# Feed-forward products as single float32 instructions in a one-core encoder layer

## The chip, the cores and the metric

The kernel runs on one NeuronCore of a Trainium2 chip. The metric is the device time of one execution in microseconds (us). TensorE (PE) multiplies matrices, VectorE (DVE), ScalarE (ACT) and GpSimd (POOL) do the rest of the arithmetic, and SyncE (SP) issues most of the transfers between device memory and the on-chip SBUF. Each engine works through its own queue in order.

## The reference

One layer of a bidirectional encoder is computed for two sequences of 1024 rows with 1024 features, all in float32. Attention (four heads with low-rank compressed queries, keys and values) and a two-dimensional Fourier mixing run side by side on one normalised input. The change lies in what follows, the gated feed-forward part:

```python
x = x + ga1 * mix
h2 = rmsnorm(x, g_ffn) * (1.0 + sc2) + sh2
ffn = (jax.nn.silu(h2 @ w_gate) * (h2 @ w_up)) @ w_down
return x + ga2 * ffn
```

`w_gate` and `w_up` are 1024 x 2816, `w_down` is 2816 x 1024. A last normalisation of the rows follows.

## The kernel before

**How a product is written.** A float32 matrix is split into a rounded half `hi` (ACT casts it to float32r, line 63) and a remainder `lo` (DVE subtracts, line 64). `mm3` (lines 78 to 81) then adds three matmuls into one PSUM bank: hi x hi, hi x lo and lo x hi. Nearly all products of the kernel are made this way. In a few places, such as `fold_out` (line 322), a product of two plain float32 tiles is one `matmul`.

**Order.** Each engine's instructions are put in order by a scheduler that follows the dependencies; `tc.issue_after` and `first` add orders by hand, and `behind()` (line 71) holds an instruction until the last split has been issued. Tiles with the same tag share memory: a load into one waits until the last reader of its predecessor has finished.

**Feed-forward (from line 1544).** Both products use a seven-product scheme on 2 x 2 blocks (Strassen's, in Winograd's form), so sums of blocks are multiplied instead of eight plain block pairs. It works in two stages for each of the two sequences.

- *Gate and up* (the loop over `order`, 22 iterations). The seven right-hand sides, `H[k]`, are blocks of the transposed input or sums of them, each 128 x 4 x 512. They stay in SBUF for the whole stage, as a hi and a lo tile. `prep_h` loads each as plain float32 into a staging tile (`HSTAGE`, line 1550) and splits it. The seven left-hand sides of an iteration come from `combos`: it loads two tiles of 512 KB from `wgu` into slots of the tag X (four of them, line 1556), and `sums_w` (line 1622) makes three new tiles and changes one in place, with four subtractions: t3, then b12 and t2, then t4. They are on POOL except in the first iterations. `hl` splits each of the seven. `prod` (line 1767) runs four `mm3` for each pair, 28 in an iteration. Between them DVE and ACT read the three PSUM banks `x`, `y` and `z` of the iteration, apply silu and multiply. `put_s` stores the results and sums of them to device memory (`s_d`); in the first sequence `down_combos` makes sums of `w_down` (`t_d`).
- *Down* (`prod2`, line 1938). Seven calls with eleven steps each. A step loads two 128 x 512 tiles into an X slot from `s_d` and from `w_down` or `t_d`, splits both, and runs four `mm3` into four banks. Between the steps, `hooks` run the residual, the last normalisation and the loads and splits of the next sequence's `H`. In the second sequence the seventh product is prepared ahead: `prep_last` loads and splits its eleven pairs into the memory of `H`, and 44 `mm3` at line 2067 follow.

That gives 2 x 22 x 28 = 1232 products in the first stage, 13 x 11 x 4 = 572 in the second and the 44 at line 2067: 1848 products of a 128 x 128 by a 128 x 512 tile.

**The entry.** While the last rows of attention's output projection run, `prep_h` loads the first `H` tiles, splits are placed among the projection's own DVE and ACT work with `issue_after` and `first` (lines 1660 to 1674), and the first weight sums go to DVE into the tile `H41`, unused at that time.

Of the kernel before, what the change touches and what calls it, by code (L numbers as in the profile page):

```python
# [12 lines left out]
F32 = mybir.dt.float32  # L13
# [8 lines left out]
P = 128  # L22
# [13 lines left out]
VALS = 18  # L36
# [17 lines left out]
def hybrid_encoder_kernel(ctx: ExitStack, tc: tile.TileContext, a: dict):  # L54
# [1489 lines left out]
    with ExitStack() as st:  # L1544
# [5 lines left out]
        HSTAGE = (("H20", "H21", "H30", "H31", "H20", "H21", "X0"), ("H20", "H21", "H30", "H31", "H30", "H20", None))  # L1550

# [3 lines left out]
        def slot(i, name="draw"):  # L1555
            return w.tile([P, 2, 512], F32, tag=f"X{i % 4}", name=name, bufs=1)


        for tag in ("H20", "X0", "X1", "H21", "H30", "H31", "H00", "H41", "H01", "H50", "H51", "H10", "H11", "H40", "H60", "H61"):
            quad(tag) if tag[0] == "H" else [slot(2 * int(tag[1]) + i) for i in range(2)]  # L1560

        def prep_h(H, s, n):

            raw = {}

            def load(i):
                k = HK[i]
                src = h2_d[s][:, HSRC[k][0] : HSRC[k][0] + 4, 512 * HSRC[k][1] : 512 * HSRC[k][1] + 512] \
                    if isinstance(HSRC[k], tuple) else hc_d[s][:, :, HSRC[k], :]
                if HSTAGE[s][i] is None:  # L1570
                    raw[k] = [val() for _ in range(4)]
                    for c in range(4):
                        nc.sync.dma_start(raw[k][c], src[:, c, :])
                elif HSTAGE[s][i] == "X0":
                    raw[k] = [slot(c, "hx") for c in range(2)]
                    for c in range(2):
                        nc.sync.dma_start(raw[k][c], src[:, 2 * c : 2 * c + 2, :])
                else:
                    t = quad(HSTAGE[s][i])
                    for c in (0, 2):  # L1580
                        nc.sync.dma_start(t[:, c : c + 2, :], src[:, c : c + 2, :])
                    raw[k] = t

            ahead = 4 if s == 0 else 3
            then = {0: 4, 1: 5, 4: 6} if s == 0 else {0: 3, 1: 5, 2: 4, 3: 6}
            for i in range(ahead):
                load(i)
                if s == 1:
                    yield
                if s == 0 and i == 0:  # L1590
                    S["rgu"] = [slot(j, "rgu0") for j in range(2)]
                    for j in range(2):
                        nc.sync.dma_start(S["rgu"][j].rearrange("p a b -> p (a b)"), a["wgu"][j, 0])
                    x3_load()
            if s == 0:
                yield
            for i, k in enumerate(HK):
                H[k] = [quad(f"H{k}{j}", F32R) for j in range(2)]
                for c in range(0, 4, n):
                    if HSTAGE[s][i] is None:  # L1600
                        for cc in range(c, c + n):
                            with behind():
                                split(H[k][0][:, cc, :], H[k][1][:, cc, :], raw[k][cc])
                    else:
                        rk = raw[k][c // 2] if HSTAGE[s][i] == "X0" else raw[k][:, c : c + n, :]
                        with behind() if s == 1 else ExitStack():
                            split(H[k][0][:, c : c + n, :], H[k][1][:, c : c + n, :], rk)
                    if c + n == 4:
                        raw.pop(k)
                        if i in then:  # L1610
                            load(then[i])
                    yield
# [44 lines left out]
        prep = prep_h(H, 0, 2)  # L1657
        next(prep)
        r, wc = S.pop("rgu"), quad("H41")
        after_a, after_v = S.pop("tail")  # L1660
        with tc.issue_after(after_a), tc.issue_after(after_v):
            next(prep)
            next(prep)
            first(here["a"], S.pop(("tail", 5)))
            first(here["v"], S.pop(("tail", 6)))
            first(here["v"], S.pop(("tail", 2)))
            first(here["v"], S["tail", 4])
            first(here["a"], S.pop(("tail", 7)))
        with tc.issue_after(S.pop(("tail", 4))):
            w0 = sums_w([r[i // 2][:, i % 2, :] for i in range(4)], lambda i: wc[:, i, :], nc.vector)  # L1670
            first(here["s"], S["tail", 3])
            with tc.issue_after(S.pop(("tail", 3))):
                next(prep)
                next(prep)
# [3 lines left out]

        def prep_step(n):
            with tc.issue_after(here["v"]):  # L1680
                for _ in range(n):
                    next(prep, None)

        for n in range(4):
# [3 lines left out]
            prep_step((2, 0, 0, 0)[n])  # L1688
            if n == 1:
                hts = quad("H40")  # L1690
# [16 lines left out]
        def hl(v):  # L1707
            h = w5.tile([P, 512], F32R, tag="wh", name="wh", bufs=8)
            if "gf" not in S:
                S["gf"] = w5.tile([P, D], F32, name="gf")  # L1710
                w5.tile([P, 2, 512], F32, tag="ga", name="tdb", bufs=1)
            l = w5.tile([P, 512], F32R, tag="wl", name="wl", bufs=8)
            split(h, l, v)
            return h, l

        gf, first_w = None, None
        order = [fi + half * (NF // 2) for fi in range(NF // 2) for half in range(2)]
        pending = []
        turn = [0]
        for s in range(2):  # L1720
            def combos(n, first=False, ahead=0):
                f = order[n]
                if first and n == 1:
                    b = [val() for _ in range(4)]
                    for i, t in enumerate(b):
                        nc.sync.dma_start(t, a["wgu"][i // 2, f][:, 4 * (i % 2) : 4 * (i % 2) + 4, :].rearrange("p c m -> p (c m)"))
                    return b
                r = [slot(turn[0] + ahead + i, "rgu") for i in range(2)]
# [3 lines left out]
                b = [r[i // 2][:, i % 2, :] for i in range(4)]  # L1732
                return b if n == 1 and s == 1 else sums_w(b, lambda i: val(), nc.vector if n == 0 else nc.gpsimd)
# [13 lines left out]
            def down_combos(f):  # L1747
                wd_ = a["w_down"]
                b1 = w5.tile([P, 2, 512], F32, tag="ga", name="tdb", bufs=1)
# [43 lines left out]
            if s == 0:  # L1793
                wts = [hl(w0[i]) for i in range(4)]
                with behind():
                    for _ in range(2):
                        next(prep)
            else:
                wts = first_w
            A = {}  # L1800
            late = None
            for n, f in enumerate(order):
                cur, nxt = wts, []
                src = combos(n + 1, s == 0 and n == 0) if n + 1 < NF else None
# [8 lines left out]
                def step(j, ps, k, first, src=src):  # L1813
                    prod(ps, k, cur[j], first)
                    if s == 0 and n == 0:
                        if j == 0:
                            cur.extend(hl(v) for v in w0[4:])
                            w0.clear()
                            S["n3"] = norm3(1, S.pop("jk3").bitcast(BF16))
                        if j < 3:  # L1820
                            with behind():
                                for _ in range(2):
                                    next(prep, None)
                            if j == 1:
                                with behind():
                                    S.pop("n3")()
                            return
                        if j == 3:
                            src = S["w1"] = sums_w(src, lambda i: val(), nc.vector)
                        src = S["w1"]  # L1830
                        for i in ((), (), (), (0, 1), (2, 3), (4,), (5, 6))[j]:
                            nxt.append(hl(src[i]))
                        if j == 6:
                            flip2(3, [S.pop(("xn", 1, 3, u)) for u in range(2)], bank, lambda g: val())
                    elif s == 1 and n == 0:
                        if j == 2:
                            with tc.issue_after(here["u2"]):
                                S["w1"] = sums_w(src, lambda i: val(), nc.vector)
                        with behind(), tc.issue_after(here["c"]) if j > 1 else ExitStack():
                            for i in ((), (), (0,), (1, 2), (3,), (4,), (5, 6))[j]:  # L1840
# [355 lines left out]
```

## Time and profile before

| | us |
|---|---|
| median of three runs | 1994.35 (1994.21 to 1997.55) |
| the profiled execution | 1991.72 |
| its span, first to last instruction | 1989.9 |
| last matmul of the projection, first of feed-forward | about 714.5 |
| last matmul of feed-forward | about 1981 |
| memory read, written | 263.01 MB, 120.65 MB |

The span is the stretch from the first to the last instruction of the profiled execution; its time has 1.8 us more around it. In the profile, a line begins with the source line, the engine, the operation, and output <- inputs. Behind the first bar of a group stands its busy time and the mean length of one instruction in ns, behind the second the idle time of the engine just before them and what ended it. A matmul is recorded as two instructions, a weight load (PEld) and the matmul proper (PE); matmul records overlap, so the pace is read from their starts.

### The profile page before, as it was taken

What the parts mean: (1) busy time and instruction counts of PE and PEld (TensorE: products, weight loads), DVE (VectorE), ACT (ScalarE), POOL (GpSimd) and SP (SyncE); (2) the same over time, 40 slices, a digit from 0 to 9 for tenths busy, and PEclk for the clock granted to TensorE, in tenths of its full rate; (3) what the DMA queues carried; (4) which work ended last, traced back from release to release, by engine and by line L of the source; (5) the groups of instructions that cost most, each with busy time, mean ns of one, the idle gap of its engine ahead of it and who ended that gap; (6) DMA issues with size and microseconds to landing.
All of it is one profiled execution on the core that took longest, in us unless ns stands there. A gap on an engine that the chain in (4) does not pass through costs nothing.

```text
span 1989.9 us, 27639 instructions
## 1 busy us (share of the span) xinstructions
PE 1965.3 (99%) x9554; PEld 1621.7 (81%) x9554; DVE 1382.5 (69%) x2081; ACT 893.7 (45%) x1743; POOL 831.0 (42%) x1008
## 2 busy tenths in 40 slices
PE   8999999999999999999999999999999999999998
PEld 6788778888888878888888888888888888888886
DVE  5667767666777687877767668779655665656794
ACT  5764545555565563333333355443333333335551
POOL 2554012111312348977877401345644544510152
PEclk9999999999999999999999999999999999999999
DMA  9986965535354584654655597774322322357762
GB/s 392 333 318 227 358 237 116 110 91 160 101 117 138 191 283 166 218 181 172 200 182 190 171 316 231 239 230 150 133 96 90 132 94 92 116 199 241 254 228 85
DMA packets 167081, 377.12 MB, mean 190 GB/s; under 512 B 18044, under 2 KB 43260, under 8 KB 163740
## 3 DMA queue, kind: packets, MB, share of 16 engines
q1 hardware_dynamic: 144252, 304.03, 45.2%
q0 software_dynamic: 22112, 70.27, 11.4%
q8 instruction: 75, 1.23, 0.2%
q10 hardware_dynamic: 576, 1.05, 0.1%
q14 instruction: 66, 0.54, 0.1%
HBM read 263.01 MB, written 120.65 MB: 193 GB/s over the span
## 4 chain that ended last, share of the span: by engine, by line
PE 59%; DVE 2%; issue 1%; POOL 1%; DMA 1%; ACT 0%; SPq 0%; POOLq 0%; DVEq 0%; ACTq 0%
PE bank L80 20%; PE bank L79 20%; PE bank L81 20%; DVE wl L64 1%; DMA draw<-in_w_down_dram 1%; DVE val L1987 0%; DVE val L154 0%; DVE val L1878 0%; DVE H L64 0%; DMA val<-x_d 0%; POOL rs_y L107 0%; POOL val L154 0%; DVE val L151 0%; POOL out_dram L1993 0%; DVE val L1875 0%
## 5 line engine op out<-in xcount | busy, mean ns | idle before, releaser
L79 PE MATMUL bank<-H,wh 128*128 128x512 f32 x1232 | 480.2, 390 | 2.6 <-DVE val L154 0.9
L80 PE MATMUL bank<-H,wh 128*128 128x512 f32 x1232 | 479.5, 389 | 0.3 <-DVE H L64 0.3
L81 PE MATMUL bank<-H,wl 128*128 128x512 f32 x1232 | 479.3, 389 | 0.2 <-DVE wl L64 0.2
L79 PEld LDWEIGHTS bank<-H,wh 128*128 128x128 f32 x1232 | 231.2, 188 | 53.2 <-DVE val L1861 2.0
L64 DVE TENSOR_TENSOR wl<-draw,wh 128x512 fp32r<-128x512 f32 x286 | 209.0, 768 | 94.0 <-ACT wh L63 93.5
L81 PEld LDWEIGHTS bank<-H,wl 128*128 128x128 f32 x1232 | 231.3, 188 | 49.0 <-DVE wl L64 0.5
L80 PEld LDWEIGHTS bank<-H,wh 128*128 128x128 f32 x1232 | 231.3, 188 | 48.2 <-DVE H L64 0.6
L154 DVE TENSOR_TENSOR val<-bank,val 128x512 f32<-128x512 f32 x200 | 136.6, 689 | 163.0 <-PE bank L81 162.1
L63 ACT CAST wh<-draw 128x512 fp32r<-128x512 f32 x286 | 164.9, 619 | 173.2 <-PE bank L80 131.6
L154 POOL TENSOR_TENSOR val<-val 128x512 f32<-128x512 f32 x58 | 82.4, 1421 | 345.7 <-DVE val L1959 163.5
L80 PE MATMUL bank<-wl,wh 128*128 128x512 f32 x572 | 223.2, 390 | 0.8 <-DVE wl L64 0.5
L63 ACT CAST wh<-rgu 128x512 fp32r<-128x512 f32 x172 | 107.1, 623 | 258.4 <-PE bank L80 203.2
L81 PE MATMUL bank<-wh,wl 128*128 128x512 f32 x572 | 222.6, 389 | 0.0
L79 PE MATMUL bank<-wh 128*128 128x512 f32 x572 | 222.6, 389 | 0.0
L63 ACT CAST wh<-val 128x512 fp32r<-128x512 f32 x133 | 82.3, 622 | 261.9 <-PE bank L80 249.3
L64 DVE TENSOR_TENSOR wl<-val,wh 128x512 fp32r<-128x512 f32 x133 | 126.1, 950 | 65.4 <-ACT wh L63 65.3
L64 DVE TENSOR_TENSOR wl<-rgu,wh 128x512 fp32r<-128x512 f32 x172 | 162.5, 945 | 0.8 <-ACT wh L63 0.7
L151 POOL TENSOR_TENSOR val<-rgu 128x512 f32<-128x512 f32 x80 | 108.3, 1354 | 78.7 <-DMA rgu<-in_wgu_dram 74.9
L80 PEld LDWEIGHTS bank<-wl,wh 128*128 128x128 f32 x572 | 107.4, 188 | 25.2 <-DVE wl L64 2.9
L79 PEld LDWEIGHTS bank<-wh 128*128 128x128 f32 x572 | 107.4, 188 | 22.5
L81 PEld LDWEIGHTS bank<-wh,wl 128*128 128x128 f32 x572 | 107.4, 188 | 21.9
L151 POOL TENSOR_TENSOR val<-val 128x512 f32<-128x512 f32 x89 | 119.1, 1356 | 1.3
(403 smaller groups left out, 3885.5 us busy)
## 6 DMA issues: line engine op xcount, KB each, us to landing
rgu<-in_wgu_dram SPq DMA_DIRECT2D x86, 512.0 KB, 4.0
draw<-s_d SPq DMA_DIRECT2D x143, 256.0 KB, 3.4
s_d<-val POOLq DMA_DIRECT2D x88, 256.0 KB, 3.0
draw<-t_d SPq DMA_DIRECT2D x88, 256.0 KB, 4.2
s_d<-val SPq DMA_DIRECT2D x66, 256.0 KB, 3.8
draw<-in_w_down_dram SPq DMA_DIRECT2D x55, 256.0 KB, 4.1
xt<-in_x_dram SPq DMA_DIRECT2D x16, 512.0 KB, 7.3
wada<-in_w_ada_dram SPq DMA_DIRECT2D x16, 512.0 KB, 9.8
```

Source lines behind the costliest of these rows:

```text
L63: here["a"] = nc.scalar.copy(hi, src).ins
L64: here["v"] = (eng or nc.vector).tensor_tensor(out=lo, in0=src, in1=rd(hi), op=ALU.subtract).ins
L79: nc.tensor.matmul(out, lh, rh, start=first, stop=False, skip_group_check=cont)
L80: nc.tensor.matmul(out, lh, rl, start=False, stop=False, skip_group_check=cont)
L81: here["t"] = here["pe"] = nc.tensor.matmul(out, ll, rh, start=False, stop=last, skip_group_check=cont).ins
L151: return eng.tensor_tensor(out=out, in0=x, in1=y, op=ALU.subtract).ins
L154: eng.tensor_tensor(out=out, in0=x, in1=y, op=ALU.add)
```

## The change

- `prod`, `prod2` and the 44 products at line 2067 issue one `nc.tensor.matmul` on plain float32 tiles instead of `mm3` on split ones.
- `hl`, `HSTAGE` and the splits of `H`, of the weight sums and of the down operands are gone, with most of the hand-made orders around them.
- `prep_h` loads each `H` tile straight into its place; `prep_last` does the same with the eleven held pairs, two in one tile.
- The freed memory goes to eight X slots (from four), 30 `val` tiles (from 18), a second tile for `tdb`, and own tiles `wc0` and `hts`.
- `combos` makes t3 and t4 on DVE, b12 and t2 on POOL, in every iteration; b11, b21, b12 and b22 are used by TensorE from the X slots themselves.

```diff
-        def prep_h(H, s, n):
+        def prep_h(H, s):
+            for k in HK:
                 src = h2_d[s][...] if isinstance(HSRC[k], tuple) else hc_d[s][:, :, HSRC[k], :]
...
+                t = H[k] = quad(f"H{k}")
+                for c in (0, 2):
+                    nc.sync.dma_start(t[:, c : c + 2, :], src[:, c : c + 2, :])
                 yield
...
-        prep = prep_h(H, 0, 2)
+        prep = prep_h(H, 0)
         next(prep)
-        r, wc = S.pop("rgu"), quad("H41")
...
+        r = [slot(j, "rgu0") for j in range(2)]
+        for j in range(2):
+            nc.sync.dma_start(r[j].rearrange("p a b -> p (a b)"), a["wgu"][j, 0])
+        x3_load()
+        for _ in prep:
+            pass
+        S.pop("tail")
+        wc = w.tile([P, 4, 512], F32, name="wc0")
...
-                r = [slot(turn[0] + ahead + i, "rgu") for i in range(2)]
+                r = [slot(turn[0] + i, "rgu") for i in range(2)]
...
-                return b if n == 1 and s == 1 else sums_w(b, lambda i: val(), nc.vector if n == 0 else nc.gpsimd)
+                b11, b21, b12, b22 = (r[i // 2][:, i % 2, :] for i in range(4))
+                t3, t2, t4 = val(), val(), val()
+                sub(t3, b22, b12, nc.vector)
+                sub(b12, b12, b11, nc.gpsimd)
+                sub(t2, b22, b12, nc.gpsimd)
+                sub(t4, b21, t2, nc.vector)
+                return [b11, t2, b21, t3, b12, t4, b22]
...
             def prod(ps, k, wt, first):
-                wh, wl = wt
                 for c in range(4):
-                    cs = slice(c * P, c * P + P)
-                    mm3(ps, wh[:, cs], wl[:, cs], H[k][0][:, c, :], H[k][1][:, c, :], first and c == 0, c == 3, not first)
+                    here["t"] = nc.tensor.matmul(ps, wt[:, c * P : c * P + P], H[k][:, c, :], start=first and c == 0, stop=c == 3,
+                                                 skip_group_check=not first).ins
...
                     nc.sync.dma_start(raw[:, 0, :], s_d[s][k, f])
                     nc.sync.dma_start(raw[:, 1, :], bsrc(k, f))
-                    ah, al = hl(raw[:, 0, :])
-                    bh, bl = hl(raw[:, 1, :])
                     for t in range(4):
-                        tt = slice(t * P, t * P + P)
-                        mm3(ps[t], ah[:, tt], al[:, tt], bh, bl, first and f == 0, last and f == NF // 2 - 1, not first)
+                        nc.tensor.matmul(ps[t], raw[:, 0, t * P : t * P + P], raw[:, 1, :], start=first and f == 0,
+                                         stop=last and f == NF // 2 - 1, skip_group_check=not first)
```

More of the change, by code (lines that the diff above doesn't have):

```diff
@@ L35 @@
 NOUT = 6
-VALS = 18
+VALS = 30
 FF = 2816
@@ L1555, in slot @@
         def slot(i, name="draw"):
-            return w.tile([P, 2, 512], F32, tag=f"X{i % 4}", name=name, bufs=1)
-        for tag in ("H20", "X0", "X1", "H21", "H30", "H31", "H00", "H41", "H01", "H50", "H51", "H10", "H11", "H40", "H60", "H61"):
-            quad(tag) if tag[0] == "H" else [slot(2 * int(tag[1]) + i) for i in range(2)]
-        def prep_h(H, s, n):
-            raw = {}
-            def load(i):
-                k = HK[i]
+            return w.tile([P, 2, 512], F32, tag=f"X{i % 8}", name=name, bufs=1)
@@ L1568, in load @@
+        for tag in ("H0", "X0", "X1", "X2", "X3", "H5", "H1", "H6", "H4", "H3", "H2", "X4", "X5", "X6", "X7"):
+            quad(tag) if tag[0] == "H" else slot(int(tag[1]))
+        def prep_h(H, s):
+            for k in HK:
                 src = h2_d[s][:, HSRC[k][0] : HSRC[k][0] + 4, 512 * HSRC[k][1] : 512 * HSRC[k][1] + 512] \
                     if isinstance(HSRC[k], tuple) else hc_d[s][:, :, HSRC[k], :]
[L1570 to L1594, printed above, removed]
@@ L1595, in prep_h @@
-            if s == 0:
-                yield
[L1597 to L1612, printed above, removed]
+                t = H[k] = quad(f"H{k}")
@@ L1677, in hybrid_encoder_kernel @@
         norm2(1, 2, 1, xb)
[L1679 to L1682, printed above, removed]
         for n in range(4):
@@ L1705, in val, with combos @@
             return w5.tile([P, 512], F32, tag="v", name="val", bufs=VALS)
[L1707 to L1714, printed above, removed]
         gf, first_w = None, None
+        S["gf"] = w5.tile([P, D], F32, name="gf")
         order = [fi + half * (NF // 2) for fi in range(NF // 2) for half in range(2)]
         pending = []
-        turn = [0]
+        turn = [4]
         for s in range(2):
-            def combos(n, first=False, ahead=0):
+            def combos(n):
                 f = order[n]
[L1723 to L1727, printed above, removed]
-                r = [slot(turn[0] + ahead + i, "rgu") for i in range(2)]
+                r = [slot(turn[0] + i, "rgu") for i in range(2)]
                 turn[0] += 2
@@ L1748, in down_combos @@
                 wd_ = a["w_down"]
-                b1 = w5.tile([P, 2, 512], F32, tag="ga", name="tdb", bufs=1)
+                b1 = w5.tile([P, 2, 512], F32, tag="tdb", name="tdb", bufs=2)
                 nc.sync.dma_start(b1, wd_[f * P : f * P + P, :].rearrange("p (a b) -> p a b", a=2))
@@ L1791, in put_s @@
                 store_s(2, fi, v4, nc.gpsimd)
[L1793 to L1799, printed above, removed]
+            wts = w0 if s == 0 else first_w
             A = {}
@@ L1802, in hybrid_encoder_kernel @@
             for n, f in enumerate(order):
-                cur, nxt = wts, []
-                src = combos(n + 1, s == 0 and n == 0) if n + 1 < NF else None
+                cur = wts
+                wts = combos(n + 1) if n + 1 < NF else None
                 if late is not None:
@@ L1811, in hybrid_encoder_kernel, with step @@
                         comb_h(1, n // 4 - 1) if n >= 5 else None
-                def step(j, ps, k, first, src=src):
+                def step(j, ps, k, first):
                     prod(ps, k, cur[j], first)
@@ L1816, in step @@
                         if j == 0:
-                            cur.extend(hl(v) for v in w0[4:])
-                            w0.clear()
                             S["n3"] = norm3(1, S.pop("jk3").bitcast(BF16))
[L1820 to L1832, printed above, removed]
+                        if j == 1:
+                            S.pop("n3")()
                         if j == 6:
                             flip2(3, [S.pop(("xn", 1, 3, u)) for u in range(2)], bank, lambda g: val())
[L1835 to L1840, printed above, removed]
-                                nxt.append(hl(S["w1"][i]))
-                        if j == 6:
-                            S.pop("w1")
-                    elif src is not None:
-                        nxt.append(hl(src[j]))
-                    if s == 0 and n == 1 and j == 2:
-                        S.pop("w1", None)
                 def pend():
                     if pending:
-                        with behind():
-                            pending.pop(0)()
+                        pending.pop(0)()
                 x, y, z = bank(), bank(), bank()
@@ L1897, in prep_last @@
             def prep_last():
-                tags = ("H00", "H01", "H50", "H51", "H10", "H11", "H60", "H61", "H40", "H41", "H30")
-                raw = {}
-                def load(f):
-                    raw[f] = quad(("H21", "H31", "H20")[f % 3])
-                    nc.sync.dma_start(raw[f][:, 0, :], s_d[1][2, f])
-                    nc.sync.dma_start(raw[f][:, 1, :], bsrc(2, f))
-                for f in range(2):
-                    load(f)
-                    yield
-                for f, tag in enumerate(tags):
-                    if f + 2 < len(tags):
-                        load(f + 2)
-                    yield
-                    q = quad(tag, F32R)
-                    for i in range(2):
-                        with behind():
-                            split(q[:, 2 * i, :], q[:, 2 * i + 1, :], raw[f][:, i, :])
-                        if i == 0:
-                            yield
-                    raw.pop(f)
-                    held.append(q)
+                for f in range(NF // 2):
+                    if f % 2 == 0:
+                        q = quad(f"H{HK[f // 2]}")
+                    v = q[:, 2 * (f % 2) : 2 * (f % 2) + 2, :]
+                    nc.sync.dma_start(v[:, 0, :], s_d[1][2, f])
+                    nc.sync.dma_start(v[:, 1, :], bsrc(2, f))
+                    held.append(v)
                     yield
@@ L1925, in hybrid_encoder_kernel @@
                 H.clear()
-            prep1 = prep_h(Hn, 1, 1) if s == 0 else prep_last()
+            prep1 = prep_h(Hn, 1) if s == 0 else prep_last()
             def put_next(f):
-                next(prep1, None)
+                if f % 2:
+                    next(prep1, None)
             wd = a["w_down"]
@@ L1936, in bsrc, with prod2 @@
                 return {0: wd[r1, :512], 1: wd[r2, :512], 2: wd[r2, 512:], 3: t_d[0, f], 4: t_d[1, f], 5: t_d[2, f], 6: t_d[3, f]}[k]
-            def prod2(ps, k, first, last, hook=None, skip=0):
+            def prod2(ps, k, first, last, hook=None):
                 for f in range(NF // 2):
-                    if f == NF // 2 - 1:
-                        turn[0] -= skip
                     raw = slot(turn[0])
-                    turn[0] += 1 + (skip if f == NF // 2 - 1 else 0)
+                    turn[0] += 1
                     nc.sync.dma_start(raw[:, 0, :], s_d[s][k, f])
                     nc.sync.dma_start(raw[:, 1, :], bsrc(k, f))
-                    ah, al = hl(raw[:, 0, :])
-                    bh, bl = hl(raw[:, 1, :])
                     for t in range(4):
-                        tt = slice(t * P, t * P + P)
-                        mm3(ps[t], ah[:, tt], al[:, tt], bh, bl, first and f == 0, last and f == NF // 2 - 1, not first)
+                        nc.tensor.matmul(ps[t], raw[:, 0, t * P : t * P + P], raw[:, 1, :], start=first and f == 0,
+                                         stop=last and f == NF // 2 - 1, skip_group_check=not first)
                     if hook is not None:
@@ L2011, in at @@
                     if todo:
-                        with behind():
-                            todo.pop(0)()
+                        todo.pop(0)()
                 return at
@@ L2017, in hybrid_encoder_kernel @@
             Y = [bank() for _ in range(4)]
-            def load_ahead(f):
-                if f in ((1, 4, 7) if s == 0 else (2, 6)):
-                    with behind():
-                        next(prep1)
-            prod2(X, 0, True, True, load_ahead)
+            prod2(X, 0, True, True)
             p1 = [val() for _ in range(4)]
@@ L2066, in hybrid_encoder_kernel @@
                     for f, q in enumerate(held):
-                        mm3(Z[t], q[:, 0, tt], q[:, 1, tt], q[:, 2, :], q[:, 3, :], False, f == NF // 2 - 1, True)
+                        nc.tensor.matmul(Z[t], q[:, 0, tt], q[:, 1, :], start=False, stop=f == NF // 2 - 1, skip_group_check=True)
                         if steps and f % 3 == 2:
@@ L2078, in first_combos @@
                 if f == NF // 2 - 2:
-                    S["w0"] = combos(0, ahead=1)
-            prod2(Z, 2, False, True, hooks(steps, first_combos), 2)
-            first_w = [hl(v) for v in S.pop("w0")]
+                    S["w0"] = combos(0)
+            prod2(Z, 2, False, True, hooks(steps, first_combos))
+            first_w = S.pop("w0")
             pending = rows_out(c11, u2, 0, 1, Z)
```

20 lines of the change are left out of this document (2 added, 18 removed).

## The prediction

> **What bounds the kernel now.** I read the busy times first, then the feed-forward stretch by stage, then the groups of matmuls, and last what TensorE waited for.
>
> ```profile
> span 1989.9 us, 27639 instructions
> PE 1965.3 (99%) x9554; PEld 1621.7 (81%) x9554; DVE 1382.5 (69%) x2081; ACT 893.7 (45%) x1743; POOL 831.0 (42%) x1008
> ...
> 714.00:1140.00 426.00, 423.51 (x1869) 1.00 0.55 188
> 1140.00:1376.00 236.00, 235.24 (x1034) 1.00 0.72 240
> 1376.00:1790.00 414.00, 413.42 (x1823) 1.00 0.36 121
> 1790.00:1982.00 192.00, 191.30 (x844) 1.00 0.63 208
> ...
> L79 PE MATMUL bank<-H,wh 128*128 128x512 f32 x1232 | 480.2, 390 | 2.6 <-DVE val L154 0.9
> L80 PE MATMUL bank<-H,wh 128*128 128x512 f32 x1232 | 479.5, 389 | 0.3 <-DVE H L64 0.3
> L81 PE MATMUL bank<-H,wl 128*128 128x512 f32 x1232 | 479.3, 389 | 0.2 <-DVE wl L64 0.2
> L80 PE MATMUL bank<-wl,wh 128*128 128x512 f32 x572 | 223.2, 390 | 0.8 <-DVE wl L64 0.5
> L81 PE MATMUL bank<-wh,wl 128*128 128x512 f32 x572 | 222.6, 389 | 0.0
> L79 PE MATMUL bank<-wh 128*128 128x512 f32 x572 | 222.6, 389 | 0.0
> ...
> L79 PE MATMUL bank<-H 128*128 128x512 f32 x44 | 17.1, 389 | 0.0
> ```
>
> The page's busy line says that TensorE works 99% of the span. The four stage rows (columns: stretch, length, TensorE busy and its instructions, granted clock, DMA share, GB/s) are the gate and up products of the first sequence, its down products, and the same for the second. TensorE is busy 1263.5 of their 1268 us, at the full clock, with the DMA engines at 36 to 72%. The matmul groups count the work: 1232 + 572 + 44 = 1848 products, each three instructions (L79, L80, L81), 5544 in all. The idle time in front of them, behind the last bar, is 2.6 + 0.3 + 0.2 + 0.8 = **3.9 us** in 1268. So nothing that feeds TensorE matters here; the end is set by how many cycles the products take. DVE and ACT, which make the split halves, are covered.
>
> **What a product costs now.** The mean of 390 ns is the length of one record, and records overlap; what counts is the distance from start to start.
>
> ```profile
> 1000.04 0.39 PE L79 MATMUL bank<-H,wh 128*128 128x512 f32 x1
> 1000.27 0.39 PE L80 MATMUL bank<-H,wh 128*128 128x512 f32 x1
> ...
> 1009.56 0.39 PE L79 MATMUL bank<-H,wh 128*128 128x512 f32 x1
> ```
>
> From 1000.04 to 1009.56 there are 42 steps (three per product, 14 products from one L79 to another): 9.52 / 42 = 0.2267 us. A product is 3 x 0.2267 = 0.680 us, and all 1848 take 1848 x 0.680 = **1256.8 us** of TensorE.
>
> **What it costs after.** The change makes each product one float32 instruction of the same shape (128x128 weights, 512 columns). The trace has that form elsewhere: `fold_out` at L322 multiplies two plain float32 tiles.
>
> ```profile
> L322 PE MATMUL bank<-wada,wuvT x8: 592/592/697, 46.0 to 52.5; 128*128 128x512 f32 x8
> ...
> L322 PE MATMUL bank<-wide,wuvT x8: 593/593/595, 55.2 to 58.2; 128*128 128x512 f32 x8
> ...
> 55.24 3.60 PE L322 MATMUL bank<-wide,wuvT 128*128 128x512 f32 x8
> ...
> 55.67 0.19 PEld L322 LDWEIGHTS bank<-wide,wuvT 128*128 128x128 f32 x1 [0.24 <-issue]
> ...
> 57.82 0.19 PEld L322 LDWEIGHTS bank<-wide,wuvT 128*128 128x128 f32 x1 [0.24 <-issue]
> ...
> L1424 PE MATMUL ppt<-ident,p 128*128 128x128 f32 x512 | 68.9, 274 | 1.4 <-DVE nb L1405 0.6
> ```
>
> Count the records against the program. `fold_out` runs for four heads and issues two matmuls for each: 8 instructions, but 8 + 8 = 16 records. The transposes at L1424 are 64 tiles x 8 = 512 instructions and 512 records, so doubling isn't a habit of the trace. **A float32 product is two records**, each with its own weight load. Their distance: eight records fill 3.60 us, the last is 0.593 us long, so (3.60 - 0.593) / 7 = 0.4296 us; the weight loads say the same, five steps from 55.67 to 57.82, 0.430 each. A product after is 2 x 0.4296 = 0.859 us, against 0.680: 26% more TensorE time for the same product. The weight load is hidden: its 0.19 us stands beside 0.43 us of matmul.
>
> 1848 x 0.8592 = **1587.8 us** instead of 1256.8: **+331.0 us**. From below, the rows bound it by their rounding: 0.01 us over five steps is 0.002 a record, 3696 records, 7 us either way. From above, if a record of two passes pays for each what a record in the dense stream pays, 2 x 0.2267 = 0.4534, the products take 3696 x 0.4534 = 1675.8 and the term is +419. I take 0.4296, the row of the very same form and shape, in a back-to-back run.
>
> A rule speaks the other way. The Trainium skill, page "Perfetto Trace Analysis", section "Engine Utilization", puts TensorE's output rate for FP32_LOW_HIGH at half of the usual. Read as the price of a whole product, 1848 x 0.43 = 794 us, that would make this change a large gain. The trace agrees for one record (0.4296 against 0.2267); that a product is two records the rule doesn't say, and there the 16 records decide. The Trainium skill's "FP8 and Floating Point Precision", section "Matmul Precision", counts four passes for true FP32, which fits two records at half rate.
>
> **What the change removes beside TensorE.** The splits:
>
> ```profile
> L64 DVE TENSOR_TENSOR wl<-draw,wh 128x512 fp32r<-128x512 f32 x286 | 209.0, 768 | 94.0 <-ACT wh L63 93.5
> ...
> L63 ACT CAST wh<-draw 128x512 fp32r<-128x512 f32 x286 | 164.9, 619 | 173.2 <-PE bank L80 131.6
> ...
> L63 ACT CAST wh<-rgu 128x512 fp32r<-128x512 f32 x172 | 107.1, 623 | 258.4 <-PE bank L80 203.2
> ...
> L63 ACT CAST wh<-val 128x512 fp32r<-128x512 f32 x133 | 82.3, 622 | 261.9 <-PE bank L80 249.3
> L64 DVE TENSOR_TENSOR wl<-val,wh 128x512 fp32r<-128x512 f32 x133 | 126.1, 950 | 65.4 <-ACT wh L63 65.3
> L64 DVE TENSOR_TENSOR wl<-rgu,wh 128x512 fp32r<-128x512 f32 x172 | 162.5, 945 | 0.8 <-ACT wh L63 0.7
> ```
>
> The three DVE groups are 497.6 us and the three ACT groups 354.3 us; all go. All lay beside TensorE, so they are worth at most the 3.9 us of idle time counted above. I take all of it: **-3.9 us**. What is late next is nothing: two of the four weight sums per iteration move from POOL to DVE, 44 x 2 x 0.69 us (the L154 operation of this shape, row below) = 61 us onto an engine that just lost 498.
>
> **The weight sums and the queues.** An iteration of gate and up is 28 products, 19.0 us now and 24.1 us after. In it DVE does t3 first, POOL two sums after it, DVE t4 last. t3 waits for the load of `rgu`; behind it in DVE's queue stand the evictions, and TensorE waits for those.
>
> ```profile
> POOL val L151 <- DMA rgu<-in_wgu_dram: 74.9, 10, 8.5
> ...
> L154 DVE TENSOR_TENSOR val<-bank,val 128x512 f32<-128x512 f32 x200 | 136.6, 689 | 163.0 <-PE bank L81 162.1
> ...
> rgu<-in_wgu_dram SPq DMA_DIRECT2D x86, 512.0 KB, 4.0
> ```
>
> Now POOL takes that wait, ten times, up to 8.5 us, where nobody needs it. After, an eviction has slack of one step, four products: 4 x 0.859 = 3.4 us. Bounds: below, nothing; above, ten waits that each pass the slack by 8.5 - 3.4 = 5.1 us, +51 us. I take nothing: the waits come from there being four X slots, two iterations' worth, and there are eight after, so a load can be issued two iterations earlier. The raw tiles are now held until their matmuls have read them, which eats one of these iterations and leaves one, 24 us, against a load of 4.0 us.
>
> **The entry.** H is loaded straight into place, seven tiles of 1 MB.
>
> ```profile
> 664.49 1.11 SPq L1581 DMA_DIRECT2D H<-h_d  x2
> ...
> 683.40 0.89 SPq L1581 DMA_DIRECT2D H<-hc_d  x2
> ...
> 696.28 2.38 SPq L1581 DMA_DIRECT2D H<-hc_d  x4
> ...
> 714.55 0.39 PE L79 MATMUL bank<-H,wh 128*128 128x512 f32 x1
> ```
>
> Those on SP's queue wait for memory that attention frees, between 664 and 696 us; the products begin at 714.55. Five tiles left at 696 at the 291 GB/s of
>
> ```profile
> 700.00:735.00 35.00, 32.06 (x151) 24.89 (x149) 30.10 (x38) 24.63 (x38) 13.43 (x23) 1.00 0.82 291
> ```
>
> need 18 us, to 714; each tile is wanted 3.4 us after the one before. Nothing, then; if memory comes free only at 714 it is some 10 us, the upper bound. The direct down-stage loads ask for 512 KB per 3.4 us, 153 GB/s, below the 240 GB/s that the second stage row moves now. The tail behind the last product stays.
>
> **Sum**, against the profiled execution: 1989.9 + 331.0 - 3.9 = 2317.0 of span. That execution took 1991.7 us, 1.8 more than its span, and the median shown is 2.6 above it: 2317.0 + 1.8 + 2.6 = **2321 us**.
>
> **The rivals.**
> 1. The float32 record is dearer in the dense stream than at L322: 0.4534 us each gives 2321 + 88 = 2409, and half of that excess 2365. For it: L322 runs at most four products in a row, with little else on the chip. Against: it alternates weights just as here, and all its steps are 0.43. Chance 0.09.
> 2. A wait replaces the split: DVE stands at t3 for `rgu` and holds the evictions, as POOL stood ten times: 2321 + 51 = 2372. For it: DVE's queue is in order. Against: twice the slots. Chance 0.13.
> 3. Faster: a product in `prod` and `prod2` is one record of 0.43 us; feed-forward then takes 794 us on TensorE and the whole some 2321 - 794 = 1527. It decides as soon as a product costs under 0.680 us. For it: two passes would be two of the present three. Against: 16 records for 8 instructions. Chance 0.03. (The Trainium skill's "Perfetto Trace Analysis", "Engine Utilization", is the rule that points here.)
> 4. The change doesn't do what it says: the operands are still treated as one-pass float32, 0.227 us a product, far faster again, near 1150 before some other engine binds. Against: the tiles are declared plain float32 as at L322. Chance 0.01.
>
> **How the numbers follow.** The forecast with its small terms (7 us of rounding either way, up to 10 us at the entry) holds from 2305 to 2335: chance 0.74. The range takes in rival 2 and the cheaper half of rival 1, and 20 us below for stalls or rounding: 2300 to 2380. A measurement here tells 0.2% (4 us) from no change. Faster has rivals 3 and 4, 0.04; within 0.2% needs a product at 0.680 by accident, 0.01; slower has the rest, 0.95.
>
> **What would show it.** The matmuls of `prod` and `prod2` should have 2 x 1848 = 3696 records, 0.43 us apart, about 593 ns each, TensorE 99% busy and the granted clock 1.00. DVE should fall to about 1382.5 - 497.6 + 61 = 946 us and ACT to 893.7 - 354.3 = 539. An up stage should last 616 x 0.859 = 529 us. The forecast is wrong if there is one record for a product, if the distance isn't 0.43, or if idle time of more than a few us stands before these matmuls, with DVE's evictions behind t3 or a load of H as releaser.

## The result, and the profile after

The changed kernel takes 2316.51 us (median of 4 runs, 2315.32 to 2319.45) against 1995.3 for the kernel before (4 runs): a ratio of **1.161**, 95% interval 1.159 to 1.163. It is slower by 321 us. The profiled execution took 2319.45 us with a span of 2317.7; 2321 was forecast, and 2317.0 for the span.

The page of the changed kernel: span and busy times, then the groups of the new matmuls with their count, busy time, mean ns and the idle time in front of them.

```profile
span 2317.7 us, 21728 instructions
## 1 busy us (share of the span) xinstructions
PE 2293.0 (99%) x7706; PEld 1284.7 (55%) x7706; DVE 910.2 (39%) x1497; ACT 513.1 (22%) x1085; POOL 675.5 (29%) x934
...
L1705 PE MATMUL bank<-H,rgu 128*128 128x512 f32 x1408 | 627.9, 593 | 2.5 <-DVE val L154 2.5
L1832 PE MATMUL bank<-draw 128*128 128x512 f32 x1144 | 491.3, 592 | 0.0
L1705 PE MATMUL bank<-H,val 128*128 128x512 f32 x1032 | 464.1, 592 | 0.0
```

DVE lost 472 us of work and ACT 381, and TensorE is as busy as before: 99%, of a longer span. L1832 is `prod2`: 572 products in the program, 1144 records. L1705 is `prod`, 1232 products: 1408 + 1032 are the two largest of its forms.

The same four stages as before (stretch, length, TensorE busy and records, granted clock, DMA share, GB/s), and below them the end of the chain that ended last (start, length, what).

```profile
714.00:1252.00 538.00, 535.49 (x1261) 1.00 0.45 160
1252.00:1516.00 264.00, 264.00 (x617) 1.00 0.58 189
1516.00:2045.00 529.00, 529.00 (x1234) 1.00 0.28 95
2045.00:2310.00 265.00, 264.25 (x616) 1.00 0.47 153
```

```profile
1516.15 528.73 PE bank L1705 x1232
2044.88 226.60 PE bank L1832 x528
2271.48 37.78 PE bank L1944 x88
2309.26 0.02 issue
```

Second-sequence gate and up is one unbroken piece: 1232 records for 616 products, 528.73 / 1232 = 0.4292 us from one to the next. The last row with matmuls is the 44 held products: 88 records, 0.429 each. Nothing but TensorE is in the chain here. The four stages lasted 1268 us before and 1596 now.

### The profile page after: what moved, and what is told of

The parts are those of the page before. It is cut to its first block, busy times and chain, and to the rows that moved or that the text cites. A ratio compares the mean times of both kernels' runs of the same rounds, so it can differ in the third digit from the quotient of the medians.

```text
span 2317.7 us, 21728 instructions
## 1 busy us (share of the span) xinstructions
PE 2293.0 (99%) x7706; PEld 1284.7 (55%) x7706; DVE 910.2 (39%) x1497; ACT 513.1 (22%) x1085; POOL 675.5 (29%) x934
## 4 chain that ended last, share of the span: by engine, by line
PE 94%; DMA 3%; ACT 1%; DVE 1%; SPq 0%; issue 0%; POOL 0%; POOLq 0%; DVEq 0%; ACTq 0%
PE bank L1705 45%; PE bank L1832 21%; PE gb L81 3%; PE gb L79 3%; PE gb L80 3%; PE bank L79 3%; PE bank L80 3%; PE bank L81 3%; PE ppt L1424 2%; PE bank L1944 2%; PE ps_s L1397 1%; PE ps_s L1399 1%; PE ps_s L1398 1%; PE ps_s L1395 1%; PE ps_s L1396 1%; DMA wide<-in_wada_dram 1%
## 5 line engine op out<-in xcount | busy, mean ns | idle before, releaser
L1705 PE MATMUL bank<-H,rgu 128*128 128x512 f32 x1408 | 627.9, 593 | 2.5 <-DVE val L154 2.5
L1832 PE MATMUL bank<-draw 128*128 128x512 f32 x1144 | 491.3, 592 | 0.0
L1705 PE MATMUL bank<-H,val 128*128 128x512 f32 x1032 | 464.1, 592 | 0.0
L1705 PEld LDWEIGHTS bank<-H,rgu 128*128 128x128 f32 x1408 | 268.0, 190 | 339.8 <-issue 331.6
L1832 PEld LDWEIGHTS bank<-draw 128*128 128x128 f32 x1144 | 217.4, 190 | 273.6 <-issue 271.2
L1705 PEld LDWEIGHTS bank<-H,val 128*128 128x128 f32 x1032 | 196.1, 190 | 246.8 <-issue 245.9
L151 POOL TENSOR_TENSOR rgu<-rgu 128x512 f32<-128x512 f32 x43 | 54.5, 1268 | 448.0 <-DVE val L151 373.4
L1404 DVE TENSOR_REDUCE mx<-ps_s 128x1 f32<-128x1024 f32 x64 | 78.1, 1220 | 43.8 <-PE ps_s L1399 43.7
L1780 DVE TENSOR_TENSOR val<-val 128x512 f32<-128x512 f32 x44 | 84.3, 1917 | 1.5
L64 DVE TENSOR_TENSOR pt<-ppt,pt 128x512 fp32r<-128x512 f32 x128 | 83.7, 681 | 2.6 <-ACT pt L63 2.4
L1409 ACT ACTIVATE p<-ps_s,nb 128x1024 f32<-128x1024 f32 x64 | 71.8, 1122 | 26.6 <-DVE nb L1405 25.8
```

The source lines that it names most:

```text
L64: here["v"] = (eng or nc.vector).tensor_tensor(out=lo, in0=src, in1=rd(hi), op=ALU.subtract).ins
L151: return eng.tensor_tensor(out=out, in0=x, in1=y, op=ALU.subtract).ins
L1404: nc.vector.tensor_reduce(out=mx, in_=ps, axis=AX.X, op=ALU.max)
L1409: nc.scalar.activation(p, ps, AF.Exp, bias=nb, scale=SCALE, accum_out=sm)
L1705: here["t"] = nc.tensor.matmul(ps, wt[:, c * P : c * P + P], H[k][:, c, :], start=first and c == 0, stop=c == 3, skip_group_check=not firs ...
L1780: nc.vector.tensor_tensor(out=u2, in0=sg, in1=u2, op=ALU.mult)
```

## The experiments

Three explanations were set against each other. **R**: a float32 product is two records of 0.43 us in place of three of 0.227, and TensorE alone sets the end. **W**: part of the loss comes from how operands are supplied: sums that moved into DVE's queue, slots held longer, loads straight into place. **P**: four passes are four passes, in whatever form they are issued.

**Four passes, each an instruction of its own.**

```diff
+    def mm4(out, lh, ll, rh, rl, first, last, cont=False):
+        nc.tensor.matmul(out, lh, rh, start=first, stop=False, skip_group_check=cont)
+        nc.tensor.matmul(out, lh, rl, start=False, stop=False, skip_group_check=cont)
+        nc.tensor.matmul(out, ll, rl, start=False, stop=False, skip_group_check=cont)
...
-                        mm3(ps[t], ah[:, tt], al[:, tt], bh, bl, first and f == 0, last and f == NF // 2 - 1, not first)
+                        mm4(ps[t], ah[:, tt], al[:, tt], bh, bl, first and f == 0, last and f == NF // 2 - 1, not first)
```

The feed-forward products of the kernel before call `mm4` in all three places; the other products keep `mm3`.

> The kernel before, with a fourth matmul, lo x lo, added to each of the 1848 feed-forward products. Theory R (TensorE alone sets the end; the price goes by how a pass is issued, 0.227 us for each float32r instruction, 0.430 for each two-pass float32 record): 1995 + 1848 x 0.2267 = 2414 us, 98 us slower than the changed kernel though both make four passes. Rival P (four passes are four passes, whatever the form): about the 2317 us of the changed kernel.

Measured: 2405.57 us, 1.206 [1.204, 1.208] of the kernel before. The timeline of this kernel (start, length, what):

```profile
1000.28 0.39 PE L87 MATMUL bank<-H,wl 128*128 128x512 f32 x1
1000.51 0.39 PE L84 MATMUL bank<-H,wh 128*128 128x512 f32 x1
1000.73 0.39 PE L85 MATMUL bank<-H,wh 128*128 128x512 f32 x1
...
1001.87 0.39 PE L86 MATMUL bank<-H,wl 128*128 128x512 f32 x1
```

The step is still (1001.87 - 1000.28) / 7 = 0.227 us. P falls: four float32r instructions cost 0.907 us a product, one float32 instruction 0.858. (R's 2414 was 8 us too high; "The rest of the sum" below says where most of that lies.) As a way to make four passes the single instruction is the cheaper one; it loses because three passes were enough.

**Only the down products, on the kernel before.**

```diff
-                    ah, al = hl(raw[:, 0, :])
-                    bh, bl = hl(raw[:, 1, :])
...
-                        mm3(ps[t], ah[:, tt], al[:, tt], bh, bl, first and f == 0, last and f == NF // 2 - 1, not first)
+                        here["t"] = here["pe"] = nc.tensor.matmul(ps[t], raw[:, 0, tt], raw[:, 1, :], start=first and f == 0,
+                                                                  stop=last and f == NF // 2 - 1, skip_group_check=not first).ins
```

> The kernel before, with only the 572 down products of prod2 made single float32 instructions on the unsplit X slots, still four of them. Theory R: 572 x (0.859 - 0.680) = +102 us, 2098 us, TensorE still without gaps. Rival W (part of the change's cost comes from how operands are supplied: slots now held until the matmuls have read them): more than 2110 us with DMA waits in front of the down matmuls.

Measured: 2092.97 us, 1.049 [1.047, 1.051]. That is +98.1 for 572 products, 0.172 each (0.179 expected; the runs of the kernel before spread over 5 us). In the groups of this kernel, the down products wait for nothing:

```profile
L1948 PE MATMUL bank<-draw 128*128 128x512 f32 x1144 | 491.3, 592 | 0.0
```

**Only the down products undone, on the changed kernel** (twelve `val` tiles fewer make room for the halves).

```diff
-VALS = 30
+VALS = 18
...
+                    ah, al = hl(raw[:, 0, :])
+                    bh, bl = hl(raw[:, 1, :])
                     for t in range(4):
-                        nc.tensor.matmul(ps[t], raw[:, 0, t * P : t * P + P], raw[:, 1, :], start=first and f == 0,
-                                         stop=last and f == NF // 2 - 1, skip_group_check=not first)
+                        tt = slice(t * P, t * P + P)
+                        mm3(ps[t], ah[:, tt], al[:, tt], bh, bl, first and f == 0, last and f == NF // 2 - 1, not first)
```

> The changed kernel, with the 572 down products of prod2 split again and in three passes (val tiles back to 18 for room). Theory R: 2316.5 - 102 = 2214 us. Rival W: the loads and sums of the changed kernel cost something of their own, so it stays above 2225 us, with gaps in TensorE.

Measured: 2216.24 us, 1.111 [1.109, 1.113]: 100.3 us less than the changed kernel. From both sides the 572 down products are worth 98 to 100 us, and what stays, 2216.24 - 1994.87 = 221.4 for the other 1276 products, is 0.173 each. All three lie a little under the 0.178 that the steps give (0.858 - 0.680), which "The rest of the sum" takes up. The cost goes with the number of products: R, with nothing left over for W, which would have made it larger.

**The splits made again, and read by nobody.**

```diff
-VALS = 30
+VALS = 18
...
+                    hl(raw[:, 0, :])
+                    hl(raw[:, 1, :])
                     for t in range(4):
                         nc.tensor.matmul(ps[t], raw[:, 0, t * P : t * P + P], raw[:, 1, :], start=first and f == 0,
```

> The changed kernel, with the splits of the down operands made again on ACT and DVE (286 casts, 286 subtractions) and read by nobody; the products stay single float32. Theory R (the splits were hidden beside TensorE and worth nothing): 2316.5 us within 4. Rival S (the split work competes with TensorE for operands or holds evictions): slower by over 10 us.

Measured: 2317.67 us (4 runs), 1.1616 [1.1597, 1.1635] against 1.161 [1.159, 1.163] for the changed kernel: no difference. Its page and its groups show that the work was there, 200 us more on DVE and 173 on ACT:

```profile
PE 2295.6 (99%) x7706; PEld 1286.1 (55%) x7706; DVE 1109.6 (48%) x1783; ACT 685.8 (30%) x1371; POOL 682.2 (29%) x934
...
L1840 PE MATMUL bank<-draw 128*128 128x512 f32 x1144 | 491.3, 592 | 0.0
```

The edit also takes the `val` tiles back to 18, to make room for the halves. The 491.3 us of the down matmuls are the same to the last digit as without the splits, and none of it is idle time. The elementwise work of the splits was worth nothing here.

**Six X slots instead of eight.**

```diff
-            return w.tile([P, 2, 512], F32, tag=f"X{i % 8}", name=name, bufs=1)
+            return w.tile([P, 2, 512], F32, tag=f"X{i % 6}", name=name, bufs=1)
```

> The changed kernel with six X slots instead of eight. Theory R (the loads have far more time than they need): 2316.5 us within 4. Rival W (DVE waits at t3 for the load, in front of the evictions, as soon as slots are short): 5.1 us for each wait that passes the slack, 22 or more of them, over 2400 us at worst; any wait of TensorE on an eviction with a load behind it would speak for it.

Measured: 2314.68 us (4 runs), 1.1606 [1.159, 1.1623]. The shortage is seen on DVE, whose waits for weight loads go from 8.8 us (two) to 18.1 us (three, the longest 10.2), but TensorE waits 0.5 us in the whole of feed-forward. W's costly form doesn't come.

**All four weight sums on POOL.**

```diff
-                sub(t3, b22, b12, nc.vector)
+                sub(t3, b22, b12, nc.gpsimd)
...
-                sub(t4, b21, t2, nc.vector)
+                sub(t4, b21, t2, nc.gpsimd)
```

> The changed kernel with all four weight sums of an iteration on POOL, as before the change, so that DVE waits for no load. Theory R: 2316.5 us within 4; the single wait of 2.5 us near 765 us, the only one before the new matmuls, may go. Rival W: the waits that the sums put into DVE's queue cost more than that, and this is faster by 5 to 50 us.

Measured: 2314.1 us (4 runs), 1.1604 [1.1586, 1.1623], 2.4 us below the changed kernel, which is inside the intervals: no difference shown. The one wait of the new matmuls on DVE is gone: its group has 2.5 us of idle time in the changed kernel and none here.

```profile
L1705 PE MATMUL bank<-H,rgu 128*128 128x512 f32 x1408 | 626.1, 592 | 0.0
...
L1705 PE MATMUL bank<-H,val 128*128 128x512 f32 x1032 | 464.2, 592 | 0.1
```

**One size changed: 256 columns instead of 512 in gate and up.** Each bank is started twice, once for each half, and the output lacks part of the sums (that the second start drops the first half's first product is the likely reason; no run separates it). The instructions and their order are what is timed.

```diff
-                    here["t"] = nc.tensor.matmul(ps, wt[:, c * P : c * P + P], H[k][:, c, :], start=first and c == 0, stop=c == 3,
-                                                 skip_group_check=not first).ins
+                    for h in (slice(0, 256), slice(256, 512)):
+                        here["t"] = nc.tensor.matmul(ps[:, h], wt[:, c * P : c * P + P], H[k][:, c, h],
+                                                     start=first and c == 0, stop=c == 3, skip_group_check=True).ins
```

> The changed kernel, with each of the 1232 gate and up products issued as two float32 instructions of 256 columns instead of one of 512: four records for a product. Theory R in its plain form (a record is two passes over its columns and next to no fixed part): 0.215 us a record, 2317 us within 5. Rival F (each record has a fixed part, as the 0.013 us by which 256-column float32r matmuls in the trace stand above half of a 512-column one would give): 2464 more records x 0.013 = +32, some 2349 us.

Measured: 2321.13 us, 1.1639 [1.1617, 1.1661]. The chain of waits in this kernel, cut to 800 to 900 us, is matmuls alone:

```profile
799.89 100.15 PE bank L1706 x464
```

100.15 / 464 = 0.2158 us a record, half of 0.4292 plus 0.0012. Twice the records cost 4.6 us by the medians, whose intervals overlap; the steps say 4928 x 0.0012 = 5.9. A float32 record is priced by its columns, and its fixed part is some 0.0025 us; rival F's 0.013 is not there. The 0.013 was itself a misreading: the 256-column float32r matmuls of the kernel before step at 0.118 us (rows in the last section), 0.005 above half of 0.2267. For a fixed part that means 0.0095 and +23 us, which is not there either.

**A try at a faster kernel: cross terms in bfloat16.** In the kernel before, gate and up:

```diff
+        nc.tensor.matmul(out, l[0], r[0], start=first, stop=False, skip_group_check=cont)
+        nc.tensor.matmul(out, l[2], r[1], start=False, stop=False, skip_group_check=cont)
+        here["t"] = here["pe"] = nc.tensor.matmul(out, l[1], r[2], start=False, stop=last, skip_group_check=cont).ins
```

`l` and `r` hold hi, lo in bfloat16, and a bfloat16 copy of the whole.

> A try at something faster than both: the kernel before, with the two cross terms of the 1232 gate and up products (hi x lo, lo x hi) made in bfloat16, from bfloat16 copies that ACT and DVE make beside the splits; hi x hi stays float32r. The cross terms are rounded, so the output is a little less exact. Theory R, if a bfloat16 pass goes at half of a float32 record, 0.2148 us: 2464 x (0.2267 - 0.2148) = -29, some 1966 us. If a bfloat16 instruction costs what a float32r one does: 1995 us, or a little more where the added copies aren't hidden.

Measured: 2004.26 us (5 runs), 1.0055 [1.0042, 1.0068]: no gain, a loss of 9.5 us. Its timeline and TensorE's waits:

```profile
999.72 0.39 PE L93 MATMUL bank<-H,wl 128*128 128x512 bf16 x1
999.95 0.38 PE L94 MATMUL bank<-H,wl 128*128 128x512 bf16 x1
999.98 0.58 PE L92 MATMUL bank<-H,wh 128*128 128x512 f32 x1
...
1003.12 0.39 PE L93 MATMUL bank<-H,wl 128*128 128x512 bf16 x1
```

```profile
PE bank L92 <- DVE val L1886: 4.3, 3, 2.4
PE bank L92 <- ACT H L84: 3.2, 1, 3.2
```

Five products from 999.72 to 1003.12 take 3.40 us, 0.680 each, as with three float32r passes. (The float32r record begins early here and is longer; only the sum of the three says something.) The copies came late in places: over the whole of feed-forward TensorE's waits add up to 10.8 us, against 3.6 by the same view in the kernel before. Between 714 and 740 us, where the entry waits, the granted clock was 0.87, against 1.00 in the kernel before. No version here beats the kernel before.

## Why the prediction was right

**The price of a product** was the term that decided, 331.0 us of it, and it came from reading two rows together: the 16 records of `fold_out`'s 8 instructions, and their distance of 0.4296 us. In the changed kernel the distance is 0.4292, so the term is 3696 x 0.4292 = 1586.3 against 1587.8. Of the bounds, the rounding of 7 us either way held, and the upper one (0.4534) was too high: a float32 record doesn't pay twice what a float32r instruction pays.

**The end set by TensorE alone.** The down products changed alone, the down products undone and the idle splits each gave what TensorE's arithmetic gives. All of the hidden work that went, 472 us on DVE and 381 on ACT, gave back no more than a few us. It was more than forecast (DVE 910 and ACT 513 us after, not 946 and 539), mostly because the sum left out the splits into the tiles `H`, 46 and 40 us in the groups of the kernel before. The -3.9 us took it that no stall would be left; 2.5 us of idle time stand before the new matmuls.

**The weight sums and rival 2.** The mechanism is there, at another place than was named, and almost free. DVE waits at t3 for a load only twice (8.8 us, at 1499 and 1506 us, ahead of the second sequence's gate and up); it waits at t4 for POOL, which the prediction didn't consider. DVE's waits in the changed kernel, and its timeline and POOL's at the only costly one:

```profile
DVE val L151 <- POOL val L151: 121.4, 43, 6.7
```

```profile
757.01 0.68 DVE L151 TENSOR_TENSOR val<-rgu 128x512 f32<-128x512 f32 x1
764.39 0.69 DVE L151 TENSOR_TENSOR val<-rgu,val 128x512 f32<-128x512 f32 x1 [6.70 <-POOL val L151]
765.00 1.28 DVE L154 TENSOR_TENSOR val<-bank,val 128x512 f32<-128x512 f32 x2
```

```profile
759.61 1.25 POOL L151 TENSOR_TENSOR tdb<-tdb 128x512 f32<-128x512 f32 x1 [3.62 <-DMA tdb<-in_w_down_dram]
761.16 0.56 POOL L1695 DMA_DIRECT2D t_d<-tdb  x1 [0.30 <-POOL tdb L151]
761.74 1.28 POOL L151 TENSOR_TENSOR rgu<-rgu 128x512 f32<-128x512 f32 x1
763.10 1.26 POOL L151 TENSOR_TENSOR val<-rgu 128x512 f32<-128x512 f32 x1
```

POOL stood at a sum of `w_down` for its load until 759.61, made b12 and t2 only then, and DVE stood at t4 for 6.70 us with two evictions behind it. TensorE waited 2.5 us. That is the slack of one step, 3.4 us, at work: of the 43 waits the other 42 are under 2.8 us each, and only the one of 6.70 reached TensorE. The price given to the rival, 51 us, took every wait as one past the slack.

**The entry** cost nothing, as forecast: SP issued the last two loads of H from 702.4 us on, and the first product began at 716.5, with no load of H among its waits. SP's queue and TensorE's timeline in the changed kernel:

```profile
702.40 1.53 SPq L1567 DMA_DIRECT2D H<-hc_d  x2
...
716.50 3.59 PE L1705 MATMUL bank<-H,rgu 128*128 128x512 f32 x8
```

**The rest of the sum.** Feed-forward lasted 716.5 to 2309.3, 1592.8 us, against 714.55 to 1981.3, 1266.8, before: +326.0 where +327.1 was forecast. That this is so close is partly luck. The price of the products gives 1586.3 - 1256.8 = +329.5. Before, feed-forward lasted 10.0 us more than its 5544 steps of 0.2267 make, and only 3.9 of them are counted as idle time; the rest is sixteen transposes (1.75 us in the changed kernel) and some 4 us in steps that are a little longer than 0.2267 here and there. After, it lasted 6.4 us more than its 3696 steps make, the stall of 2.5 included. So 3.6 us went, close to the 3.9 of the forecast, but made up otherwise. In the four-pass kernel the same excess is 3.6 us (716.67 to 2396.03, against 7392 x 0.2267), which is most of what that forecast was too high by. The 2.0 us by which feed-forward began later were there long ahead of any instruction of the change: the first matmul of `fold_out` stands at 46.05 us before and 48.09 after, and of the five variants of the changed kernel four begin feed-forward between 714.0 and 714.7, one at 716.4. Together that is the span, 0.7 us above the forecast. The median came out 4.5 us below 2321, because the profiled execution of before stood 2.6 us below its median and that of after 2.9 above its own: an execution's offset doesn't carry over.

**Rival 3** (one record for a product) would have given 1527 us. The counts ruled it out: 1144 records for 572 products. Rival 1 fell with 0.4292, and rival 4 with it.

## What to carry to other kernels

Where TensorE sets the end, price a change of number format by the distance between its records and by records per instruction, both taken from a row of the same shape; the instruction count of the source, here one for three, says the opposite of the time. A single float32 matmul makes fewer instructions, no splits and frees half of the operands' memory, and it costs 26% more than three float32r matmuls: it suits a stage where DVE, ACT or memory is short and TensorE isn't. Work taken off engines that TensorE covers is worth no more than what TensorE loses beyond its steps, here 3.9 us counted as idle time and a few more in stretched steps, and the rows say so before anything is built.

## What the runs showed of the hardware

A pass costs less inside a float32 record than as an instruction. Taken as two passes over 512 columns, as the prediction took it, the record has 0.4292 / 2 = 0.2146 us for a pass, against 0.2267 for a float32r instruction, in the four-pass kernel too. The difference of 0.012 us isn't a fixed cost of any record, since float32 records of 256 columns, with as many column passes as a 512-column float32r instruction, cost 0.2158.

Two sizes of each form divide a step into a part for the columns and a fixed part. The kernel before has float32r matmuls of 256 columns in a stretch at a granted clock of 1.00, and the changed kernel has plain float32 transposes of 128 columns:

```profile
136.93 0.28 PE L81 MATMUL bank<-wcs_h,eol 128*128 128x256 f32 x1
...
139.41 0.28 PE L81 MATMUL bank<-wcs_h,eol 128*128 128x256 f32 x1
```

```profile
726.79 1.91 PE L1603 MATMUL bank<-ident,xn 128*128 128x128 f32 x16
728.54 7.03 PE L1705 MATMUL bank<-H,rgu 128*128 128x512 f32 x16
```

From 136.93 to 139.41 there are 21 float32r steps, 0.118 us each. With 0.2267 for 512 columns the fixed part is 2 x 0.118 - 0.2267, some 0.01 us; for float32 records it is 2 x 0.2158 - 0.4292 = 0.0024. So some 0.007 of the 0.012 us is a larger fixed part of the float32r instruction. Why it has one was not settled. Sixteen transposes, one record each, take 728.54 - 726.79 = 1.75 us, 0.109 a step, which is what the float32 records' two sizes give for 128 columns.

Two things don't explain it as far as they were tried. Smaller elements didn't help: three passes of which two were bfloat16 kept the 0.680 us of a product, though what a bfloat16 pass costs by itself wasn't measured. The recorded length of the weight load doesn't follow the price either: 0.19 us stands beside the float32r and the float32 matmuls alike, and loads of 0.10 us in front of the bfloat16 matmuls left the product at 0.680.

The Trainium skill's "TensorE: Matmul & The Clock Gate", section "Back-to-back issue gap", gives N / 2.4 + 2.5 ns for an isolated matmul on a warm clock, and about 131 ns for each matmul of N = 512 in a stream of weight loads and matmuls. With the columns of two passes put in for N, which is this text's reading, the float32 record agrees with the first: 429.2 ns by the formula and 429.2 measured for 1024 column passes, 215.8 and 215.8 for 512. The float32r step of 512 columns, 226.7 ns measured in such a stream, agrees with neither 215.8 nor 131.
